# The convolution's result in two parts from where it is made to where it is used

## The chip, the cores and the metric

One core of one Trainium2 chip runs the whole program. The metric is the device time of one execution in microseconds (us); the smaller it is, the better. Matrix products run on TensorE (PE in the profile), elementwise work on VectorE (DVE) and ScalarE (ACT), and SyncE (SP) issues most transfers; ACT issues some too.

## The reference, cut to what matters

One encoder layer (model width 1024) is applied to two sequences of 1024 positions, the prompt and the sample, each with its own conditioning vector. A sequence is normed and projected to twelve operands; a gated short convolution gives `y_a`, a two-way gated linear attention with four heads gives `y_b`, and the two are merged under sigmoid gates:

```
proj = h @ w_in
(a_b, a_c, a_x, a_z, q, k, v, b_z, lr_f, lr_b, m_a, m_b) = split(proj)
u   = depthwise_conv(a_c * a_x, conv_w, conv_b)          # three taps
y_a = (a_b * u * silu(a_z)) @ w_a_out                    # <- the convolution's result is a_b * u * silu(a_z)
y_b = (attention(q, k, v, gates) * silu(b_z)) @ w_b_out
out = x + gate * ((sigmoid(m_a) * y_a + sigmoid(m_b) * y_b) @ w_out)
```

All of it is float32. The kernel does a product as three products of rounded parts: an operand is split in a high part, rounded to the format that TensorE multiplies (`F32R`), and the low part that is left, and hi*hi + hi*lo + lo*hi is summed.

## The kernel before

Work goes sequence by sequence: `projections(0)`, `mixers(0)`, a merge, then `projections(1)`, `mixers(1)` and the second merge. Everything is kept with features on the 128 partitions and the 1024 positions beside each other, in rows of 128x1024 (512 KB); a product is made in halves of 512 positions.

In `projections` the convolution's eight rows are made. Two rows at a time come out of four jobs (`conv_jobs`); the first row (`first_conv`, sequence 0 only) and the single ones (`last_conv_jobs`) are made apart. A job does a block of 256 features with seven block products instead of eight (`fast`), of 12 matmuls each, and in sequence 0 the weights' seven operands are made on the way: ACT casts the high part, DVE subtracts it for the low one, and one operand is a sum of two blocks (line 204 to 208: `s` by DVE, its high part by ACT, its low part by DVE). When a convolution row `u` is finished by its last multiplication (line 646, 669 or 746), ACT's queue stores it, unsplit, in the DRAM tensor `ta_d[s][ct]` (lines 647, 670, 747).

In `mixers` each of four heads goes through `attention`. Its first part is a chain over levels B = 1, 2, 4, ..., 64. At a level ACT copies the keys into `km` (line 931), PE makes 16 small products `pl<-Q,km` (line 903; the program has 8 instructions, the profile counts two for each), DVE copies those that a mask names into `AT` (line 936; ACT from B = 32 on, lines 940 and 941), and DVE multiplies `Q` (944), `K` (947) and `T` (949) by the level's decays. The next level's `km` needs the new `K`, its products also the new `Q`.

Between the steps of this chain a generator of dense products is advanced, `gates()` and then `first_out()`. The last group of `gates()` is two blocks of the merge gate, 96 matmuls in eight steps k. From k = 4 on, each step calls `reload`, which brings two rows of the convolution's result back: four loads of 256 KB (a half row each) into staging slots `raw` by the SP queue (line 117), and for each a cast `b<-raw` by ACT (line 122) and a subtraction `b<-raw,b` by DVE (line 123). A tile `b` holds the high and the low part of a row in one of 18 big slots (1 MB). `first_out()` is the product with `w_a_out`: 12 matmuls for each `b` in its first group (`ps<-b,w`, lines 141 to 143). The first group's four result banks are those of the gate's last group; ACT's sigmoids (line 764) free them.

The order on every engine is decided when the kernel is built by a scheduler with its own estimates; on the chip each engine works its list in order, and waits at an instruction whose operands are not there.

Of the kernel before, what the change touches and what calls it, by code (L numbers as in the profile page):

```python
# [11 lines left out]
F32 = mybir.dt.float32  # L12
F32R = mybir.dt.float32r
# [4 lines left out]
P = 128  # L18
D = 1024
KT = D // P  # L20
L = 1024
# [36 lines left out]
def encoder_kernel(ctx, tc, x_p, x_s, x_t, weights, w_lr, w_gate, w_out, vectors, b_gate, final_norm_g, masks, y_p, y_s):  # L58
    nc = tc.nc
# [9 lines left out]
    dram = ctx.enter_context(tc.tile_pool(name="dram", bufs=1, space=bass.MemoryType.DRAM))  # L69


    def big(name, dtype=F32, shape=(P, 2, L)):
        return sb.tile(list(shape), dtype, name=name, tag="big", bufs=NBIG)
# [29 lines left out]
    kept_d = dram.tile([36, 7, P, 2 * HALF], F32, name="kept_d")  # L103
    g_d = [dram.tile([2 * KT, P, L], F32, name=f"g_d{s}") for s in range(2)]
    m1_d = [dram.tile([KT, P, L], F32, name=f"m1_d{s}") for s in range(2)]
    ta_d = [dram.tile([KT, P, L], F32, name=f"ta_d{s}") for s in range(2)]
    ob_d = [dram.tile([KT, P, L], F32, name=f"ob_d{s}") for s in range(2)]
    mg_d = [dram.tile([P, KT, L], F32, name=f"mg_d{s}") for s in range(2)]
    r1_d = dram.tile([P, L], F32, name="r1_d")
# [7 lines left out]
        queue(nc.sync.dma_start(out=raw, in_=src))  # L117
        return raw

    def split(hi, lo, raw, engine):  # L120

        high = nc.scalar.copy(out=hi, in_=raw)  # L122
        engine.tensor_sub(out=lo, in0=raw, in1=hi.bitcast(F32))  # L123
        return high

    def load_w(i, w=None, **kw):
# [469 lines left out]
    def projections(s, mv, started):  # L596
        def tile_of(kind):

            made = {}

            def place(r, c):
                sl = slice(c * HALF, (c + 1) * HALF)
                if kind == "big":
                    if "t" not in made:
                        made["t"] = big("pair")
                    return made["t"][:, r, sl]
                if r not in made:
                    made[r] = small("single")
                return made[r][:, sl]

            return place

        whole = slice(0, L)

        def taps(ct, pr):

            w = [vecs[:, V_CW + 8 * i + ct:V_CW + 8 * i + ct + 1] for i in range(3)]
            u = small("u")
            nc.scalar.activation(out=u, in_=pr, func=AF.Identity, scale=w[1], bias=vecs[:, V_CB + ct:V_CB + ct + 1])
            for i, src, dst in ((0, slice(0, L - 1), slice(1, L)), (2, slice(1, L), slice(0, L - 1))):  # L620
                nc.vector.scalar_tensor_tensor(out=u[:, dst], in0=pr[:, src], scalar=w[i], in1=u[:, dst],
                                               op0=ALU.mult, op1=ALU.add)
            return u

        def row(place, r):
            a = place(r, 0)
            return bass.AP(a.tensor, a.offset, [list(a.ap[0]), [1, L]])

        def silu(z, sg):
            nc.scalar.activation(out=sg, in_=z, func=AF.Sigmoid)  # L630
            nc.vector.tensor_mul(out=z, in0=z, in1=sg)

        def conv_jobs(ct):
            pc, px, pz, pb = tile_of("big"), tile_of("big"), tile_of("small"), tile_of("small")
            us = {}

            def x_there(r):
                nc.vector.tensor_mul(out=row(pc, r), in0=row(pc, r), in1=row(px, r))
                us[r] = taps(ct + r, row(pc, r))

            def z_there(r):
                silu(row(pz, r), row(px, r))
                nc.vector.tensor_mul(out=us[r], in0=us[r], in1=row(pz, r))

            def b_there(r):
                nc.vector.tensor_mul(out=us[r], in0=us[r], in1=row(pb, r))
                nc.scalar.dma_start(out=ta_d[s][ct + r], in_=us[r])

            return [pair(w + ct, w + ct + 1, p, there) for w, p, there in (
                (W_AC, pc, lambda r: None), (W_AX, px, x_there), (W_AZ, pz, z_there), (W_AB, pb, b_there))]  # L650

        def last_conv_jobs(ct):

            p1, p2 = tile_of("big"), tile_of("big")
            u, done = [], []

            def cx_there(r):
                done.append(r)
                if len(done) == 2:
                    nc.vector.tensor_mul(out=row(p1, 0), in0=row(p1, 0), in1=row(p1, 1))  # L660
                    u.append(taps(ct, row(p1, 0)))

            def zb(r):
                done.append(r)
                if r == 0:
                    silu(row(p2, 0), row(p1, 1))
                    nc.vector.tensor_mul(out=u[0], in0=u[0], in1=row(p2, 0))
                if len(done) == 4:
                    nc.vector.tensor_mul(out=u[0], in0=u[0], in1=row(p2, 1))
                    nc.scalar.dma_start(out=ta_d[s][ct], in_=u[0])  # L670

            return [pair(W_AC + ct, W_AX + ct, p1, cx_there), pair(W_AZ + ct, W_AB + ct, p2, zb)]

        def out_job(i, dst, gate=None):

            p = tile_of("small")

            def there(r):
                if gate == "silu":
                    silu(row(p, r), small("sg"))  # L680
                elif gate:
                    nc.scalar.activation(out=row(p, r), in_=row(p, r), func=AF.Sigmoid)
                nc.scalar.dma_start(out=dst[r], in_=row(p, r))

            load, place, quarter = pair(i, i + 1, p, there)
            if W_V <= i < W_BZ:
                load.load = lambda n, kh: value_tile(i, n, kh)
            return load, place, quarter

        jobs = []  # L690
        if started:
            first_conv(s, mv, started, taps, silu)
        for ct in range(1, 7, 2):
            jobs += conv_jobs(ct)
        jobs += last_conv_jobs(KT - 1)
        n_conv = len(jobs)

        for w, d in ((W_Q, q_d), (W_K, k_d)):
            jobs.append(out_job(w, [d[s][r, :, 0, :] for r in range(2)]))
        for g in range(NH):  # L700
            jobs.append(out_job(W_V + 2 * g, [v_d[s][g, :, r, :] for r in range(2)]))
            jobs.append(out_job(W_BZ + 2 * g, [z_d[s][g, :, r, :] for r in range(2)], "silu"))
        for f in range(0, KT, 2):
            jobs.append(out_job(W_MA + f, [g_d[s][f + r] for r in range(2)], "sigmoid"))
        for n, (load, _, _) in enumerate(jobs):
            load.keep, load.ready, load.even = n, s == 1, n >= n_conv
        if not started:
            more = last_conv_jobs(0)
            jobs = more + jobs
            n_conv += len(more)  # L710
        steps = 7 * (len(jobs) - n_conv)
        side = chain(decays(s), gate_rows() if s else ())
        n_side = (1 + 9 * NH) + (KT + 1 + 2 if s else 0)
        owed = 0.0
        for n, _ in enumerate(fast(jobs, mv)):
            if s and n == 8:
                run(low_ranks(s, mv))
            if n + 1 >= 7 * n_conv:
                owed += 1.02 * n_side / steps
                while owed >= 1.0:  # L720
                    owed -= 1.0
                    next(side, None)
        run(side)

    def first_conv(s, mv, started, taps, silu):

        banks, sums_of = started
        pr, zs = small("pr"), [small("z") for _ in range(2)]
        z, sg = zs
        for ps, sl in banks[0]:  # L730
            nc.scalar.copy(out=pr[:, sl], in_=ps)
        for ps, sl in banks[1]:
            nc.vector.tensor_mul(out=pr[:, sl], in0=ps, in1=pr[:, sl])
        for ps, sl in banks[2]:
            nc.scalar.copy(out=z[:, sl], in_=ps)
        pb = small("pb")
        more = chain(halves(W_AB, lambda ps, sl: nc.scalar.copy(out=pb[:, sl], in_=ps), mv.act), low_ranks(s, mv))
        next(more)
        for k in range(4):
            sums_of(k)  # L740
            next(more, None)
        run(more)
        u = taps(0, pr)
        silu(z, sg)
        nc.vector.tensor_mul(out=u, in0=u, in1=z)
        nc.vector.tensor_mul(out=u, in0=u, in1=pb)
        nc.scalar.dma_start(out=ta_d[s][0], in_=u)
        mf = small("mf", shape=(P, len(MASKED), P))
        nc.sync.dma_start(out=mf, in_=masks)
        nc.vector.tensor_copy(out=mk, in_=mf)  # L750


    def mixers(s, mv):
        def gates():
# [18 lines left out]

            for k, _ in enumerate(group([(W_MA + i, gate(i)) for i in range(n, n + 2)], mv.act)):
                if k >= 4:
                    reload(ta_d[s], conv, (2 * k - 8, 2 * k - 7))
                yield

        conv = [None] * KT
# [360 lines left out]
    mv = Moving()  # L1140
    started = start(mv)
    projections(0, mv, started)
    mixers(0, mv)
    mv = Moving()
# [73 lines left out]
```

## Time and profile before

| | |
|---|---|
| median of 3 runs | 2373.42 us (2373.26 to 2377.82) |
| the profiled execution | 2377.87 us, span 2376.0 us |
| PE busy | 2301.9 us, 97% of the span |
| DVE busy | 1424.6 us, 60% |
| ACT busy | 1008.8 us, 42% |
| memory traffic | 294.90 MB read, 197.79 MB written, 207 GB/s over the span |

The span runs from the first to the last instruction; the time of the execution has 1.9 us more around it. A busy share close to one on PE means that time is lost or won almost only where PE stands, or where its clock is lower.

### The profile page before, as it was taken

How to read it: one execution, taken by the hardware profiler on the slowest of the kernel's cores; microseconds unless marked ns; L12 is line 12 of the kernel's file. 1: busy time of each engine (PE TensorE's matmuls, PEld its weight loads, DVE VectorE, ACT ScalarE, POOL GpSimd, SP SyncE). 2: the span in 40 equal slices, each digit the busy share in tenths (PEclk: the TensorE clock that was granted, in tenths of full speed). 3: DMA queues.
4: the chain of work that ended last, by engine and by line, in shares of the span. 5: the costliest groups of instructions: out<-in, count | busy, mean ns of one | idle time of the engine just before them, and what ended most of it. 6: DMA issues, size and time to landing. Idle time of an engine off the chain costs nothing.

```text
span 2376.0 us, 29248 instructions
## 1 busy us (share of the span) xinstructions
PE 2301.9 (97%) x10897; PEld 1883.3 (79%) x10897; DVE 1424.6 (60%) x2021; ACT 1008.8 (42%) x1655; POOL 34.3 (1%) x72
## 2 busy tenths in 40 slices
PE   7999999999999989999999999999999989999998
PEld 3688887887888868878788888888778878888887
DVE  4676676666576878868622332344476876965443
ACT  4443443666655546443421112555145544442221
POOL 0000000000000000000000000000000000000000
PEclk8999999999999999999999999999999999999999
DMA  6267767888863245557366667787853244478431
GB/s 234 71 245 282 268 252 279 314 298 302 308 235 110 99 146 201 211 184 245 113 202 212 212 201 230 256 277 269 306 187 113 101 150 169 160 246 300 154 124 62
DMA packets 189902, 494.63 MB, mean 208 GB/s; under 512 B 18912, under 2 KB 45632, under 8 KB 185664
## 3 DMA queue, kind: packets, MB, share of 16 engines
q1 hardware_dynamic: 166960, 405.98, 49.8%
q10 hardware_dynamic: 22800, 86.78, 9.4%
q8 instruction: 86, 1.41, 0.2%
q14 instruction: 56, 0.46, 0.1%
HBM read 294.90 MB, written 197.79 MB: 207 GB/s over the span
## 4 chain that ended last, share of the span: by engine, by line
PE 83%; DMA 7%; DVE 6%; ACT 2%; issue 1%; POOL 1%; SPq 0%; POOLq 0%; DVEq 0%; ACTq 0%
PE ps L141 9%; PE ps L143 9%; PE ps L142 9%; PE pl L277 8%; PE pl L278 8%; PE pl L279 8%; PE ps L278 6%; PE ps L279 6%; PE ps L277 6%; PE pl L903 3%; DMA raw<-in_weights_dram 2%; DMA qk<-q_d 2%; PE pm L141 1%; PE pm L142 1%; PE pm L143 1%
## 5 line engine op out<-in xcount | busy, mean ns | idle before, releaser
L123 DVE TENSOR_TENSOR w<-raw,w 128x512 fp32r<-128x512 f32 x298 | 202.2, 686 | 100.1 <-ACT w L122 99.1
L122 ACT CAST w<-raw 128x512 fp32r<-128x512 f32 x298 | 183.3, 621 | 161.7 <-PE ps L143 51.5
L277 PE MATMUL pl<-th,w 128*128 128x512 f32 x584 | 228.1, 391 | 1.1 <-ACT keep L282 1.1
L278 PE MATMUL pl<-tl,w 128*128 128x512 f32 x584 | 227.9, 390 | 0.0
L279 PE MATMUL pl<-th,w 128*128 128x512 f32 x584 | 227.6, 390 | 0.0
L141 PE MATMUL ps<-b,w 128*128 128x512 f32 x512 | 202.8, 396 | 0.4 <-ACT w L122 0.3
L142 PE MATMUL ps<-b,w 128*128 128x512 f32 x512 | 201.8, 394 | 0.2 <-DVE b L123 0.2
L143 PE MATMUL ps<-b,w 128*128 128x512 f32 x512 | 201.0, 393 | 0.0
L141 PE MATMUL ps<-hi,w 128*128 128x512 f32 x432 | 173.5, 402 | 1.7 <-ACT hi L390 1.7
L143 PE MATMUL ps<-hi,w 128*128 128x512 f32 x432 | 171.2, 397 | 1.5 <-DVE w L123 1.5
L142 PE MATMUL ps<-lo,w 128*128 128x512 f32 x432 | 170.7, 395 | 0.7 <-DVE lo L391 0.7
L282 ACT COPY keep<-pl 128x512 f32<-128x512 f32 x116 | 67.7, 584 | 242.2 <-PE pl L279 242.1
L278 PE MATMUL ps<-lo,w 128*128 128x512 f32 x352 | 138.2, 393 | 0.4 <-DVE lo L123 0.4
L279 PE MATMUL ps<-hi,w 128*128 128x512 f32 x352 | 137.8, 391 | 0.4 <-DVE w L123 0.4
L277 PE MATMUL ps<-hi,w 128*128 128x512 f32 x352 | 137.7, 391 | 0.3 <-ACT hi L122 0.3
L277 PEld LDWEIGHTS pl<-th,w 128*128 128x128 f32 x584 | 110.0, 188 | 24.9 <-ACT keep L282 1.7
L278 PEld LDWEIGHTS pl<-tl,w 128*128 128x128 f32 x584 | 109.9, 188 | 23.0
L279 PEld LDWEIGHTS pl<-th,w 128*128 128x128 f32 x584 | 109.8, 188 | 22.9
L903 PE MATMUL pl<-Q,km 128*128 128x128 f32 x768 | 101.8, 287 | 19.4 <-ACT km L931 14.5
L903 PEld LDWEIGHTS pl<-Q,km 128*128 128x128 f32 x768 | 95.3, 198 | 31.5 <-ACT km L931 20.1
L141 PEld LDWEIGHTS ps<-b,w 128*128 128x128 f32 x512 | 97.0, 189 | 19.3 <-ACT w L122 0.7
L142 PEld LDWEIGHTS ps<-b,w 128*128 128x128 f32 x512 | 96.9, 189 | 19.0 <-DVE b L123 1.0
(287 smaller groups left out, 5043.7 us busy)
## 6 DMA issues: line engine op xcount, KB each, us to landing
kept_d<-w SPq DMA_DIRECT2D x196, 512.0 KB, 4.1
raw<-in_weights_dram SPq DMA_DIRECT2D x256, 256.0 KB, 4.3
w<-kept_d SPq DMA_DIRECT2D x112, 512.0 KB, 3.4
wk<-kept_d SPq DMA_DIRECT2D x168, 256.0 KB, 3.1
g<-g_d SPq DMA_DIRECT2D x32, 512.0 KB, 4.6
araw<-in_weights_dram SPq DMA_DIRECT2D x16, 512.0 KB, 3.7
ta_d<-u ACTq DMA_DIRECT2D x16, 512.0 KB, 3.5
v_d<-single ACTq DMA_DIRECT2D x16, 512.0 KB, 5.2
```

What stands on the lines that cost most here:

```text
L122: high = nc.scalar.copy(out=hi, in_=raw)
L123: engine.tensor_sub(out=lo, in0=raw, in1=hi.bitcast(F32))
L141: nc.tensor.matmul(out, ahi, bhi, start=(first and i == 0), stop=False)
L142: nc.tensor.matmul(out, ahi, blo, start=False, stop=False)
L143: nc.tensor.matmul(out, alo, bhi, start=False, stop=(last and i == n - 1))
L277: nc.tensor.matmul(ps, whi[:, cs], mhi, start=(first and k == 0), stop=False, skip_group_check=True)
L278: nc.tensor.matmul(ps, whi[:, cs], mlo, start=False, stop=False, skip_group_check=True)
L279: nc.tensor.matmul(ps, wlo[:, cs], mhi, start=False, stop=(k == 3), skip_group_check=True)
L282: nc.scalar.copy(out=job[i, "keep"], in_=ps)
L903: nc.tensor.matmul(pl[:, j * P:(j + 1) * P], km[:, c * P:(c + 1) * P], qm(c), start=True, stop=True)
```

## The change

A row of the convolution's result is split at once where it is made: `keep_conv` lets ACT cast `u` into a spare row (one whose contents are used up: `z`'s row of the pair, or of the single row), lets DVE subtract the cast from `u` in place, and stores both, the high part and the low one, by two 512 KB transfers on ACT's queue. `ta_d` has two parts for each row. Where the row is wanted again, one 1 MB load on SP's queue brings both parts into a `b` tile; there is no staging slot, no cast and no subtraction.

```diff
-    ta_d = [dram.tile([KT, P, L], F32, name=f"ta_d{s}") for s in range(2)]
+    ta_d = [dram.tile([KT, 2, P, L], F32, name=f"ta_d{s}") for s in range(2)]
...
-    def split(hi, lo, raw, engine):
+    def split(hi, lo, raw, engine, hi32=None):
 
         high = nc.scalar.copy(out=hi, in_=raw)
-        engine.tensor_sub(out=lo, in0=raw, in1=hi.bitcast(F32))
+        engine.tensor_sub(out=lo, in0=raw, in1=hi.bitcast(F32) if hi32 is None else hi32)
         return high
...
+        def keep_conv(ct, u, spare):
+
+            split(spare.bitcast(F32R), u.bitcast(F32R), u, nc.vector, hi32=spare)
+            for i, t in enumerate((spare, u)):
+                nc.scalar.dma_start(out=ta_d[s][ct, i], in_=t)
...
             def b_there(r):
                 nc.vector.tensor_mul(out=us[r], in0=us[r], in1=row(pb, r))
-                nc.scalar.dma_start(out=ta_d[s][ct + r], in_=us[r])
+                keep_conv(ct + r, us[r], row(pz, r))
...
-                    nc.scalar.dma_start(out=ta_d[s][ct], in_=u[0])
+                    keep_conv(ct, u[0], row(p2, 0))
...
-        nc.scalar.dma_start(out=ta_d[s][0], in_=u)
+        keep_conv(0, u, z)
...
                 if k >= 4:
-                    reload(ta_d[s], conv, (2 * k - 8, 2 * k - 7))
+                    for f in (2 * k - 8, 2 * k - 7):
+                        conv[f] = big("b", F32R)
+                        nc.sync.dma_start(out=conv[f].bitcast(F32), in_=ta_d[s][f].rearrange("a p t -> p a t"))
                 yield
```

The scheduler places the rest anew. Lines below the diff's first insertion have other numbers in the changed kernel (903 becomes 911, 931 becomes 939, 764 becomes 770). PE's list at the third head's levels, where the convolution's rows come back, in the kernel before: behind the last products of the gate's group (`ps<-hi,w`, `ps<-lo,w`) stand the 24 of levels B = 4, 8 and 16 together, then the first ones with `b`.

```order
L141 MATMUL ps<-hi,w 128x512
L142 MATMUL ps<-lo,w 128x512
L143 MATMUL ps<-hi,w 128x512
L903 MATMUL pl<-Q,km 128x128 x24
L141 MATMUL ps<-b,w 128x512
L142 MATMUL ps<-b,w 128x512
```

The same place in the changed kernel, from the products of B = 4 on:

```order
L911 MATMUL pl<-Q,km 128x128 x8
L141 MATMUL ps<-hi,w 128x512
L142 MATMUL ps<-lo,w 128x512
L143 MATMUL ps<-hi,w 128x512
L141 MATMUL ps<-hi,w 128x512
L142 MATMUL ps<-lo,w 128x512
L143 MATMUL ps<-hi,w 128x512
L911 MATMUL pl<-Q,km 128x128 x8
L141 MATMUL ps<-b,w 128x512
L142 MATMUL ps<-b,w 128x512
L143 MATMUL ps<-b,w 128x512
```

Six matmuls of the gate's group now stand between B = 4 and B = 8; behind B = 8 come five with `b` (the last two, lines 141 and 142, are not shown), and then the eight of B = 16. It is the same in both sequences.

ACT's list at that place, before: `Xh` is the cast that opens the chain, `sg` are the gate's sigmoids that free PE's banks.

```order
L122 CAST Xh<-K 128x2048
L122 CAST b<-raw 128x512 x5
L913 COPY K<-qk 128x1024
L924 COPY AT<-pl 128x512 x2
L122 CAST b<-raw 128x512
L931 COPY km<-K 128x1024
L122 CAST b<-raw 128x512 x4
L931 COPY km<-K 128x1024
L122 CAST b<-raw 128x512 x4
L931 COPY km<-K 128x1024
L122 CAST b<-raw 128x512 x2
L931 COPY km<-K 128x1024
```

And now:

```order
L122 CAST w<-raw 128x512 x2
L122 CAST Xh<-K 128x2048
L921 COPY K<-qk 128x1024
L932 COPY AT<-pl 128x512 x2
L939 COPY km<-K 128x1024 x2
L122 CAST w<-raw 128x512 x2
L939 COPY km<-K 128x1024 x2
L770 ACTIVATE sg<-ps 128x512 x3
```

The 16 casts of `b` are gone, and four casts of the first weights of `w_a_out`, which stood behind the last `km` before, stand ahead. DVE's list loses its 16 subtractions for `b` there in the same way, and SP's list has eight loads `b<-ta_d` in place of sixteen `raw<-ta_d`, six of these slots' early turns being taken by weights.

DVE's list at the first convolution row of sequence 0, before, from the row's last multiplication on:

```order
L746 TENSOR_TENSOR u<-u,pb 128x1024
L123 TENSOR_TENSOR w<-raw,w 128x512
L204 TENSOR_TENSOR s_838<-raw 128x512
L289 TENSOR_TENSOR pair<-ps,keep 128x512
L206 TENSOR_TENSOR raw<-raw 128x512
L208 TENSOR_TENSOR w<-s_838,w 128x512
```

And now:

```order
L752 TENSOR_TENSOR u<-u,pb 128x1024
L123 TENSOR_TENSOR w<-raw,w 128x512
L204 TENSOR_TENSOR s_841<-raw 128x512
L123 TENSOR_TENSOR u<-u,z 128x1024
L206 TENSOR_TENSOR raw<-raw 128x512
L289 TENSOR_TENSOR pair<-ps,keep 128x512
L207 TENSOR_TENSOR raw<-s_841,raw 128x512
L292 TENSOR_TENSOR pair<-pl,pair 128x512
L208 TENSOR_TENSOR w<-s_841,w 128x512
```

The subtraction that makes the convolution row's low part, a full row, is in, and line 208, which makes the low part of a weights' operand, stands three instructions later.

## Rows read from the trace of the kernel before

**Rows 1.** PE's waits over the span: total us, times, longest.

```profile
PE pl L903 <- ACT km L931: 14.5, 6, 6.3
```

**Rows 2.** By tile, `b` and `ta_d`: ns min/median/max of both splits; who waited for loads.

```profile
L122 ACT CAST b<-raw x64: 610/618/661, 861.2 to 2124.1; 128x512 fp32r<-128x512 f32 x64
L123 DVE TENSOR_TENSOR b<-raw,b x64: 678/690/708, 863.5 to 2124.7; 128x512 fp32r<-128x512 f32 x64
...
  ACT b L122: 21.4, 14
```

**Rows 3.** PE's timeline, sequence 0, third head: start, duration, [idle before <-releaser].

```profile
873.64 0.39 PE L143 MATMUL ps<-hi,w 128*128 128x512 f32 x1
874.98 2.05 PE L903 MATMUL pl<-Q,km 128*128 128x128 f32 x16 [0.95 <-ACT km L931]
883.31 3.79 PE L903 MATMUL pl<-Q,km 128*128 128x128 f32 x16 [6.28 <-ACT km L931]
889.22 2.59 PE L903 MATMUL pl<-Q,km 128*128 128x128 f32 x16 [2.12 <-DVE Q L944]
891.46 0.77 PE L141 MATMUL ps<-b,w 128*128 128x512 f32 x1
...
893.74 0.47 PE L143 MATMUL ps<-b,w 128*128 128x512 f32 x1
```

**Rows 4.** ACT's timeline at the same place.

```profile
877.04 0.62 ACT L122 CAST b<-raw 128x512 fp32r<-128x512 f32 x1 [2.12 <-DMA raw<-ta_d]
...
882.22 1.04 ACT L931 COPY km<-K 128x1024 f32<-128x1024 f32 x1
...
889.25 1.56 ACT L764 ACTIVATE sg<-ps 128x512 f32<-128x512 f32 x3
```

**Rows 5.** DVE's timeline at the same place.

```profile
875.30 1.90 DVE L123 TENSOR_TENSOR b<-raw,b 128x512 fp32r<-128x512 f32 x3
877.11 1.34 DVE L936 COPY_PREDICATED AT<-mk,pl 128x512 f32<-128x512 uint8 x2
878.33 1.23 DVE L944 TENSOR_TENSOR Q<-Q,T 128x1024 f32<-128x1024 f32 x1
879.46 1.30 DVE L947 TENSOR_TENSOR K<-K,T 128x512 f32<-128x512 f32 x2
```

**Rows 6.** PE's timeline, sequence 1, third head, the same three levels.

```profile
1944.06 2.05 PE L903 MATMUL pl<-Q,km 128*128 128x128 f32 x16 [1.24 <-ACT km L931]
1951.10 3.78 PE L903 MATMUL pl<-Q,km 128*128 128x128 f32 x16 [4.99 <-ACT km L931]
1957.01 2.02 PE L903 MATMUL pl<-Q,km 128*128 128x128 f32 x16 [2.12 <-ACT w L122]
```

**Rows 7.** PE's timeline in sequence 0's projections, a wait and a matmul behind it.

```profile
414.67 0.70 PE L862 MATMUL pm<-lrs,wg 96*128 96x512 f32 x2 [2.23 <-DMA lrs<-lr_d]
...
416.18 0.63 PE L278 MATMUL ps<-lo,w 128*128 128x512 f32 x1
```

**Rows 8.** Windows: us, PE, PEld, DVE, ACT, POOL busy (count), PEclk, DMA share, GB/s.

```profile
200.00:300.00 100.00, 100.00 (x443) 82.83 (x442) 64.00 (x90) 37.34 (x62) 0.00 (x0) 1.00 0.75 275
...
884.25:886.50 2.25, 2.25 (x13) 2.25 (x12) 1.12 (x3) 0.97 (x2) 0.00 (x0) 0.50 0.97 258
...
1060.00:1080.00 20.00, 19.96 (x89) 16.17 (x88) 11.74 (x18) 5.05 (x9) 0.00 (x0) 1.00 0.93 327
```

**Rows 9.** First convolution row: DVE makes an operand's low part; PE's first use.

```profile
132.94 0.68 DVE L208 TENSOR_TENSOR w<-s,w 128x512 fp32r<-128x512 f32 x1
...
135.29 0.39 PE L279 MATMUL ps<-th,w 128*128 128x512 f32 x1
```

**Rows 10.** The same two instructions at a later pair of convolution rows.

```profile
205.99 0.68 DVE L208 TENSOR_TENSOR w<-s,w 128x512 fp32r<-128x512 f32 x1
...
211.45 0.39 PE L279 MATMUL ps<-th,w 128*128 128x512 f32 x1
```

**Rows 11.** PE's use of `vT`, third head of sequence 0: ns, first and last start.

```profile
L961 PE MATMUL pm<-ident,vT x16: 272/272/328, 907.7 to 911.7; 128*128 128x128 f32 x16
```

More of the change, by code (lines that the diff above doesn't have):

```diff
@@ L691, in projections @@
         if started:
-            first_conv(s, mv, started, taps, silu)
+            first_conv(s, mv, started, taps, silu, keep_conv)
         for ct in range(1, 7, 2):
@@ L723, in projections, with first_conv @@
         run(side)
-    def first_conv(s, mv, started, taps, silu):
+    def first_conv(s, mv, started, taps, silu, keep_conv):
         banks, sums_of = started
```

## The prediction

> **What bounds the kernel now.** The busy table comes first: PE is at work for 97% of the span, so other engines count only where PE stands. The list of PE's waits says where. Its largest entry is the products of the attention's levels waiting for ACT's copy `km`: 14.5 us in six waits [rows 1]. PE's timeline puts 13.5 of these 14.5 us at one place in each sequence, the first part of the third head, where the convolution's rows are loaded back. In sequence 0, PE waits 0.95, 6.28 and 2.12 us before levels B = 4, 8 and 16, which is 9.35 us [rows 3]; in sequence 1 it waits 1.24, 4.99 and 2.12, which is 8.35 us [rows 6].
>
> Next to read is what else PE loses there: its clock. Sixteen level products take 2.05 us at their best and 3.79 after the 6.28 us wait [rows 3], and the granted clock of that stretch is 0.50, the lower level, 1.2 GHz [rows 8]. Over sequence 0 that costs 3.79 - 2.05 = 1.7, then 2.59 - 2.05 = 0.5, then the first six matmuls with `b`: the last of them starts 2.28 us after the first [rows 3], against 5 x 0.226 = 1.13 at the usual spacing (100 us for 443 matmuls, [rows 8]), 1.1 more. Together 3.4 us. In sequence 1 it is 3.78 - 2.05 = 1.7 [rows 6].
>
> Last, the timelines of the two engines that the chain runs through. ACT's shows why `km` is late: casts `b<-raw` stand in front of it, and such a cast waits for its load [rows 4]; in all, ACT's casts for `b` wait 21.4 us, in 14 waits, for loads from `ta_d` [rows 2]. DVE is never idle long there, and subtractions for `b` stand between the level's own operations: three of them between 875.30 and 877.11, ahead of the copies into `AT` [rows 5]. So both engines of the chain are held up by the split on loading. The place costs 9.35 + 3.4 = 12.8 us in sequence 0 and 8.35 + 1.7 = 10.1 in sequence 1.
>
> **What is removed.** Per sequence, 16 casts of 0.62 us and 16 subtractions, which follow each other at (877.11 - 875.30) / 3 = 0.60 us [rows 5], 9.7 us of DVE time in a chain that is served by DVE and ACT in turn. The Trainium skill ("VectorE: DVE Perf Modes", the section on the TRN2 errata) says that an instruction pays a fixed time on top of its elements, which would make 512 elements 0.69 us. That is the duration in the row of the split, 0.69 [rows 2], but instructions queued behind each other start 0.60 us apart, so the spacing is what I count; by the page's figure the sum would free 11.1 us instead of 9.7 on DVE, and the chain below would be no shorter for it, as it counts only its own operations.
>
> **What the chain needs without them**, sequence 0, on the same clock times. PE's list now holds six of the gate's matmuls back until after B = 4, so PE comes to B = 4 at 873.64 + 0.23 - 6 x 0.226 = 872.5. Before, `km` for it was copied behind three waiting casts; with these and four subtractions (2.4 us) out of the way I count it as ready, no wait. The products take 2.05, to 874.6; the six matmuls cover PE to 875.9. In that time DVE has a half of the copies (0.61), `Q` (878.33 to 879.46, 1.13) and the second half of `K` (0.60) to do [rows 5], 2.34, to 876.9; then ACT's copy takes 1.04 [rows 4], and with two handovers of about 0.1 the products of B = 8 start at 878.1. **PE waits 2.2 us.** They end at 880.2. Next come five matmuls with `b`; their first bank is freed by the gate's first sigmoid, which ACT's list has behind the `km` of B = 16. That `km` waits for DVE: two weights' subtractions, `T` and two halves of `K` behind 876.9, 3.0 us, to 879.9; copy to 881.0; a third of 1.56 us for the first sigmoid [rows 4], 881.5. **PE waits 1.4 us.** The five take 1.1, to 882.7; B = 16 then finds its `Q` (879.9 + 1.22 + 1.13 = 882.3) and ends at 884.8. Before, PE was as far (B = 16 and five with `b` issued) at 893.74 [rows 3]. That is 8.9 us earlier.
>
> From this comes what the clock takes. A single wait of 2.23 us in the projections was followed by matmuls of 0.63 us instead of 0.39 [rows 7]; the 3.78 and 2.05 us of [rows 6] differ by 1.7 behind 4.99 us. I take 1.7 per sequence, with nothing and 3.4 as its ends. **Sequence 0 gains 8.9 - 1.7 = 7.2 us. Sequence 1** has the same order; it keeps 2.2 + 1.4 + 1.7 = 5.3 of its 10.1, **a gain of 4.8.**
>
> **The loads.** Eight of 1.05 MB instead of sixteen of 256 KB: 8.4 MB, twice the bytes. Their slots come free one after another; the latest is last read in the gate's step k = 5, and 24 matmuls follow that step, so it is free by 873.9 - 24 x 0.226 = 868.5 at the latest. At 327 GB/s, the rate of a stretch with the DMA engines busy 0.93 [rows 8], 8.4 MB take 25.7 us; even if nothing moved before 868.5 all is there by 894.2. PE wants the first `b` at 881.6 and each further one 12 x 0.226 = 2.7 us later, the eighth after 900. On the same bound the first lands at 871.7 (1.05 MB, 3.2 us). No wait, with 6 us in hand or more. At the 258 GB/s of the slow stretch [rows 8] the eight take 32.5 us, to 901: the eighth is then the first that could be late.
>
> **What is added in the projections.** For each of the 16 rows a cast of 1024 (ACT's copy of that size is 1.04, [rows 4]), a subtraction of 1024 (`Q` of that size 1.13 to 1.23, [rows 5]) and a second 512 KB store, with ACT's queue standing until the subtraction is done. PE has no idle there and DVE 36 us free of 100 [rows 8], so what matters is whether a weights' operand comes late. At the first row it does: the low part of the operand ends at 132.94 + 0.68 = 133.62 and is wanted at 135.29 [rows 9], 1.67 in hand; the full subtraction (1.13) and two 0.60 instructions now stand ahead of it, 2.33 us. **0.7 lost.** At the pairs there is 211.45 - 206.67 = 4.8 in hand [rows 10], against two subtractions, 2.3, and ACT held for about 1.9 (one of them and an instruction of 0.69 ahead of it): hidden, but with half a microsecond to spare if both add up. The extra 4.2 MB of stores in about 350 us are 12 GB/s on 275 [rows 8]. I put 1.0 for all of this, 0.7 and 3 as its ends.
>
> **Sum:** 7.2 + 4.8 - 1.0 = **11.0 us**. The profiled execution took 2377.87, at the upper end of the three runs, and would take 2366.9; from the median of 2373.42 it is **2362.4 us**. A measurement of this kernel can tell about 0.2%, 4.7 us, from no change.
>
> **Rivals.**
> - *All of the place is won* (12.8 + 10.1 - 1.0 = 21.9, 2351.5). It wants the DVE chain to keep ahead of PE at B = 8, which six matmuls (1.36 us) don't cover by the count above. 0.12.
> - *The wait stays in the chain.* Levels alternate PE, DVE, ACT, PE, and if the copies of B = 2 still come late, B = 4 waits 1.5 us more, B = 8 runs at the lower clock and with it `b`: 3.6 + 1.5 + 3.4 = 8.5 is left of each sequence, the gain 4.3 + 1.6 - 1.0 = 4.9, 2368.5; anything worse is within the bound. The 2.34 us of DVE operations per level, which the change doesn't touch, speak for it; the 21.4 us of waiting casts, which are gone, against. 0.16.
> - *SP's queue.* The loads of `g` (two of 512 KB) and `vT` (1 MB) now stand behind 8.4 MB. The Trainium skill ("DMA: Bandwidth & Descriptors", on queues, rings and completion order) has a DMA engine take a queue's work in the order of its ring; no row of before tests that. In rows: behind loads that end at 894.2 by the bound above, `vT` lands 2 x 3.2 later, at 900.6 at 327 GB/s; its first use, at 907.7 [rows 11], moves to 900.5 by the 7.2 us gained. The bound starts all eight loads at the last one's time; by the order six of the slots are free a step of 12 matmuls (2.7 us) sooner at least, which I take to leave it in time. At 258 GB/s from 2.7 us sooner it is 868.5 - 2.7 + 32.5 + 2 x 4.1 = 906.5, PE stands 6 us in sequence 0 and as long in sequence 1, and of the 11.0 gained nothing is left: 2374. 0.06.
> - *Slower: the projections' operands come late at the pairs.* With more than 4.8 us of added delay there PE waits, and what comes next is a clock drop. Were the six pair rows of sequence 0 late by 2.2 us each, as in [rows 7], with 1.6 of clock behind it (eight matmuls of twice the spacing), 6 x 3.8 = 23 us would be lost: 2362.4 + 23 = 2385. It becomes slower than before from 1.8 us a row on. For it speaks that ACT's list is in order and stands behind the second store; against it the 36% that DVE has free. 0.06.
>
> **The chances.** The forecast has 0.60, and its own range is 2357 to 2368: the ends of the clock (1.7 each way and sequence) and of the projections' 1.0. With the full gain on one side and the chain's wait on the other the range is **2351 to 2371**. Faster by over 0.2% (below 2368.7) are the forecast, the full gain and half of the third case: 0.80. Within 0.2%: the rest of it and the queue, 0.14. Slower by over 0.2%: 0.06.
>
> **What would show it.** In the changed kernel's trace PE should have no wait before B = 4, one of about 2 us before B = 8 put down to `km`, and one of 1 to 2 us before the first `b`, put down to a sigmoid; ACT's waits for `ta_d` should be gone, and PE should not wait for `b`'s loads. In the projections one new wait of about 0.7 us at an operand of line 208 near 135 us. I am wrong if PE waits over 3 us at B = 4 or B = 8, if it waits for loads of `b` or `vT`, or if more than a microsecond or two of new waits stand in the first 600 us.

## The result, and the profile after

The changed kernel takes 2356.57 us (median of 4, 2353.4 to 2362.86) against 2375.53 of the kernel before on the same chip: a ratio of 0.9922, 95% interval 0.9907 to 0.9937, 18.5 us faster. Two later comparisons of the same pair gave 0.9936 (0.9923 to 0.9949) and 0.9928 (0.9912 to 0.9945), 15 and 17 us. The profiled execution took 2362.86 us with a span of 2361.1, where the one of before had 2376.0: 14.9 us, and it is the slowest of the four. Two more executions of the changed kernel were profiled with the later comparisons, with spans of 2355.4 and 2357.2; of the kernel before there is the one.

PE's waits over the span: total us, times, longest.

```profile
PE pm L1054 <- DVE ot L1046: 11.6, 16, 2.5
PE pl L911 <- ACT km L939: 6.0, 4, 2.5
```

The 14.5 us of [rows 1] are 6.0 now. What was the second entry, the 16 waits for `ot` in the attention's last part, which the change doesn't touch, is the first. PE's timeline at the third head of sequence 0 shows levels B = 4 and 8, the first `b` and B = 16:

```profile
874.01 1.95 PE L911 MATMUL pl<-Q,km 128*128 128x128 f32 x16
879.82 3.61 PE L911 MATMUL pl<-Q,km 128*128 128x128 f32 x16 [2.48 <-ACT km L939]
883.26 0.50 PE L141 MATMUL ps<-b,w 128*128 128x512 f32 x1
...
885.46 2.02 PE L911 MATMUL pl<-Q,km 128*128 128x128 f32 x16 [0.79 <-DVE Q L952]
```

Against [rows 3], the waits are 0, 2.48 and 0.79 us instead of 0.95, 6.28 and 2.12. The sixteen products of B = 8 take 3.61 us, 1.6 over their 2.05. The same place in sequence 1, B = 8, the first `b` and B = 16 (B = 4 doesn't wait):

```profile
1939.52 2.05 PE L911 MATMUL pl<-Q,km 128*128 128x128 f32 x16 [2.48 <-ACT km L939]
1942.96 0.50 PE L141 MATMUL ps<-b,w 128*128 128x512 f32 x1 [1.38 <-ACT sg L770]
...
1944.22 1.95 PE L911 MATMUL pl<-Q,km 128*128 128x128 f32 x16
```

The same wait of 2.48 us before B = 8, but here its products run at full speed (2.05), and the wait for the sigmoid before the first `b` shows, 1.38. In sequence 0 the slow products hid it, and the later `Q` took its place. The third profiled execution bears this out: there the products of B = 8 take 2.05 us in sequence 0 too, and the wait for the sigmoid shows, 1.38. DVE's timeline there, sequence 0, behind the products of B = 4, answers to [rows 5]:

```profile
875.65 1.34 DVE L944 COPY_PREDICATED AT<-mk,pl 128x512 f32<-128x512 uint8 x2
876.88 1.21 DVE L952 TENSOR_TENSOR Q<-Q,T 128x1024 f32<-128x1024 f32 x1
878.01 0.68 DVE L955 TENSOR_TENSOR K<-K,T 128x512 f32<-128x512 f32 x1
```

and ACT's, for [rows 4]:

```profile
878.73 1.04 ACT L939 COPY km<-K 128x1024 f32<-128x1024 f32 x1 [0.73 <-DVE K L955]
```

Copies, `Q` and `K` follow each other on DVE with nothing between; `km` waits for `K` alone, and starts right behind it, at 878.73 where `K` ends at 878.69.

The waits don't tell all that the place gained. PE issues the same instructions there before and after, so the stretch from the first products of the third head's B = 2 to those of the fourth head's can be compared whole (us, then the busy time and the count of PE, PEld, DVE, ACT and POOL, granted clock, DMA share, GB/s). Before, sequence 0 and 1:

```profile
867.96:981.77 113.81, 99.89 (x534) 84.30 (x534) 93.74 (x146) 61.89 (x120) 2.40 (x4) 0.96 0.63 220
1936.87:2038.94 102.07, 92.07 (x505) 77.02 (x505) 80.95 (x125) 48.45 (x98) 2.40 (x4) 0.97 0.55 196
```

And after:

```profile
869.54:974.84 105.30, 97.94 (x534) 82.56 (x534) 84.09 (x130) 54.91 (x108) 2.40 (x4) 0.98 0.70 258
1929.26:2023.42 94.16, 89.27 (x505) 75.51 (x505) 71.22 (x109) 41.67 (x86) 2.40 (x4) 1.00 0.62 235
```

The two stretches fell from 215.9 us to 199.5, and to 198.6 and 198.4 in the two other profiled executions: 16.4 to 17.5 us are won there.

The loads in transfers: the window from 858 to 905 us in 40 slices of 1.2 us.

```profile
GB/s 244 0 0 12 225 356 415 408 429 415 429 404 418 404 404 418 404 418 394 401 425 401 401 363 373 436 429 418 418 411 451 364 282 94 0 0 14 37 197 174
```

They move at 363 to 451 GB/s in an unbroken stretch, 409 in the mean from 866 to 891 us, and PE waits for none. In sequence 0's projections PE has one new wait and a longer one (windows 60 to 200 us and 200 to 420):

```profile
PE ps L279 <- DVE w L208: 0.6, 1, 0.6
...
PE pm L870 <- DMA lrs<-lr_d: 3.1, 1, 3.1
```

The first is the operand at the first row. The second was 2.2 us before. All of PE's waits from 60 to 700 us are 10.0 us, and 9.4 and 9.8 in the other two profiled executions, where they were 8.0.

### The profile page after: what moved, and what is told of

Its sections match the earlier page's. It is cut to its first block, busy times and chain, and to the rows that moved or that the text cites. A ratio compares the mean times of both kernels' runs of the same rounds, so it can differ in the third digit from the quotient of the medians.

```text
span 2361.1 us, 29175 instructions
## 1 busy us (share of the span) xinstructions
PE 2296.8 (97%) x10897; PEld 1878.6 (80%) x10897; DVE 1423.5 (60%) x2005; ACT 1006.6 (43%) x1639; POOL 34.3 (1%) x72
## 4 chain that ended last, share of the span: by engine, by line
PE 82%; DMA 6%; DVE 5%; ACT 3%; issue 2%; SPq 1%; POOL 1%; POOLq 0%; DVEq 0%; ACTq 0%
PE ps L141 10%; PE ps L143 10%; PE ps L142 10%; PE pl L277 8%; PE pl L278 8%; PE pl L279 8%; PE ps L279 6%; PE ps L278 6%; PE ps L277 6%; PE pl L911 3%; DMA raw<-in_weights_dram 2%; PE pm L141 1%; DMA qk<-q_d 1%; PE pm L142 1%; PE pm L143 1%
## 5 line engine op out<-in xcount | busy, mean ns | idle before, releaser
L141 PEld LDWEIGHTS ps<-b,w 128*128 128x128 f32 x512 | 96.3, 188 | 21.0 <-ACT sg L770 1.6
L142 PEld LDWEIGHTS ps<-b,w 128*128 128x128 f32 x512 | 96.3, 188 | 18.6 <-DVE b L123 0.5
L143 PEld LDWEIGHTS ps<-b,w 128*128 128x128 f32 x512 | 96.3, 188 | 18.6
```

The source lines that it names most:

```text
L141: nc.tensor.matmul(out, ahi, bhi, start=(first and i == 0), stop=False)
L142: nc.tensor.matmul(out, ahi, blo, start=False, stop=False)
L143: nc.tensor.matmul(out, alo, bhi, start=False, stop=(last and i == n - 1))
```

## The experiments

The theory behind the prediction is that the split on loading held the level chain on both engines. The rivals: only ACT's casts with their waits for loads did; only DVE's time did; or PE's new list did, which the scheduler wrote anew when the split was gone.

**The changed kernel again**, two more times beside the others.

> The changed kernel once more, on the same chip as the three others, to size the differences: 15 us under the kernel before if the two profiled executions are right (span 2361.1 against 2376.0), 19 if the medians of four are.

> The changed kernel a third time, beside the two others: 0.992 to 0.995 of the kernel before.

Measured 0.9936 and 0.9928; the intervals are given above. The three comparisons agree within them; single executions differ by up to 12 us (2353.4 to 2365.7 over all of them), and so a difference of a few us between kernels is read from the trace rather than from one median: from waits, and from the two stretches of the third head where the work is the same.

**DVE's operations put back.**

```diff
                         nc.sync.dma_start(out=conv[f].bitcast(F32), in_=ta_d[s][f].rearrange("a p t -> p a t"))
+                        for t in range(2):
+                            lo = conv[f][:, 1, t * HALF:(t + 1) * HALF]
+                            nc.vector.tensor_tensor(out=lo, in0=lo.bitcast(F32), in1=lo.bitcast(F32), op=ALU.max)
```

> The changed kernel with DVE's time put back: each loaded b gets two DVE operations of 512 on its low part (a maximum of the part with itself, which changes nothing), 16 per sequence, in the places where the subtractions stood; ACT has no cast for b. PE's list is again that of the kernel before (17 matmuls of the gate's group, then the levels B = 4 and 8 together), as the scheduler reacts to DVE's load. Theory 1 (the level chain was held by both engines' work): DVE's 9.6 us per sequence in the chain make PE wait some 3 us at B = 4 and 5 at B = 8, most of the gain goes, 2364 to 2371. Theory 2 (only ACT's casts, which waited for loads in front of km, held the chain): DVE's operations fit in beside, PE's waits stay near those of the changed kernel, 2355 to 2360.

Measured: 2373.89 us, ratio to the kernel before 0.9985 (0.9974 to 0.9995). Of the gain 3.6 us (1.2 to 6.2) are left. PE's timeline, B = 4, B = 8 and the first `b` of sequence 0:

```profile
876.72 2.05 PE L914 MATMUL pl<-Q,km 128*128 128x128 f32 x16 [1.66 <-ACT km L942]
883.54 3.79 PE L914 MATMUL pl<-Q,km 128*128 128x128 f32 x16 [4.77 <-ACT km L942]
888.79 0.79 PE L141 MATMUL ps<-b,w 128*128 128x512 f32 x1 [1.46 <-ACT sg L770]
```

DVE and ACT of the same kernel in front of B = 8:

```profile
876.94 1.93 DVE L787 TENSOR_TENSOR b<-b 128x512 fp32r<-128x512 f32 x3
878.74 1.36 DVE L947 COPY_PREDICATED AT<-mk,pl 128x512 f32<-128x512 uint8 x2
881.09 1.32 DVE L958 TENSOR_TENSOR K<-K,T 128x512 f32<-128x512 f32 x2
...
882.44 1.04 ACT L942 COPY km<-K 128x1024 f32<-128x1024 f32 x1 [5.77 <-DVE K L958]
```

PE's waits are 1.66 + 4.77 + 1.46 = 7.9 us in sequence 0 (9.35 before), and the same in sequence 1. ACT has no casts for `b`, and stands idle 5.77 us for `K`. The two stretches of the third head, with as many PE instructions as above, take together:

```profile
sum 215.47, PE 193.91 PEld 163.30 DVE 173.56 ACT 96.58 POOL 4.79; mean PE 96.95 PEld 81.65 DVE 86.78 ACT 48.29 POOL 2.40
```

That is 215.5 us against 215.9 in the kernel before. DVE's operations alone bring the loss back. "Only ACT" falls.

**ACT's copies put back.**

```diff
                         nc.sync.dma_start(out=conv[f].bitcast(F32), in_=ta_d[s][f].rearrange("a p t -> p a t"))
+                        for t in range(2):
+                            hi = conv[f][:, 0, t * HALF:(t + 1) * HALF]
+                            nc.scalar.copy(out=hi, in_=hi.bitcast(F32))
```

> The changed kernel with ACT's work put back: each loaded b gets two ACT copies of 512 on its high part (already rounded, so they change nothing), 16 per sequence, which wait for the loads and stand partly in front of km as the casts did; DVE has no subtraction for b, and PE's list is nearly that of the changed kernel (six gate matmuls between B = 4 and 8, one with b between B = 8 and 16). Theory 1 (both engines held the chain): 16 x 0.52 = 8.3 us of ACT, of which some six copies (3 us) and their waits stand in front of the km of B = 4 and 8; 3 to 6 us per sequence lost, 2362 to 2368. Theory 2 (only ACT held it): all of the gain goes, 2370 to 2375. Theory 3 (DVE's time alone, and PE's list, made the gain): 2355 to 2359, as the changed kernel.

Measured: 0.9936 (0.9920 to 0.9953), the same as the changed kernel beside it, 0.9936. PE before B = 8 and B = 16, sequence 0, and ACT in front of the `km` of B = 8:

```profile
877.42 3.56 PE L914 MATMUL pl<-Q,km 128*128 128x128 f32 x16 [2.69 <-ACT km L942]
883.00 2.02 PE L914 MATMUL pl<-Q,km 128*128 128x128 f32 x16 [1.78 <-DVE Q L955]
...
875.29 1.13 ACT L787 CAST b<-b 128x512 fp32r<-128x512 f32 x2
876.33 1.04 ACT L942 COPY km<-K 128x1024 f32<-128x1024 f32 x1
```

The wait at B = 8 is 0.2 us longer than in the changed kernel, since two copies end just behind `K`; the waits of the place are 4.5 us in sequence 0 against 3.3. The two stretches take together:

```profile
sum 201.51, PE 187.79 PEld 159.28 DVE 155.48 ACT 111.69 POOL 4.81; mean PE 93.90 PEld 79.64 DVE 77.74 ACT 55.84 POOL 2.40
```

That is 2 to 3 us more than the changed kernel's 198.4 to 199.5, for 15 us more of ACT's work, and part of it is the clock, which was low behind B = 8 in both sequences; it doesn't show in the time of the execution. The theory that both engines' work held the chain asked 3 to 6 us per sequence, and falls at that price. One thing this run doesn't bring back is the casts' waiting: the whole rows had landed, and ACT waited 0.2 us for loads in all, against 21.4 in [rows 2]. What that waiting did can only be read from the kernel before. In sequence 0, DVE's `K` for B = 8 ends at 879.46 + 1.30 = 880.76 [rows 5], and `km` starts at 882.22 [rows 4], behind casts that had waited:

```profile
881.05 1.26 ACT L122 CAST b<-raw 128x512 fp32r<-128x512 f32 x2 [1.41 <-DMA raw<-ta_d]
```

So ACT's casts held `km` up by 1.5 us beyond `K` there, and by 0.4 us at the same level of sequence 1; at B = 4 it was 0.1 and 0.3. They ended about when DVE did, and might have held the chain nearly as long by themselves. No run has these waits without DVE's operations, and so this rival is left open.

**The list on PE without DVE's time.** DVE's operations and PE's old list came together, so the list was put back by itself, by priority for the last two steps of the gate's group:

```diff
+            def ahead(steps):
+                k = 0
+                while True:
+                    if k >= 6:
+                        with tc.high_priority(offset=100):
+                            go = next(steps, 1)
...
-            for k, _ in enumerate(group([(W_MA + i, gate(i)) for i in range(n, n + 2)], mv.act)):
+            for k, _ in enumerate(ahead(group([(W_MA + i, gate(i)) for i in range(n, n + 2)], mv.act))):
```

> The changed kernel with another list on PE and no added work: the last two steps of the gate's group are given priority, so that no gate matmul is left between B = 4 and B = 8 (18 stand ahead of B = 4, and its products and those of B = 8 follow each other, as in the kernel before). DVE has no operations for b. It tells DVE's time from PE's list, which came together in the run with DVE's operations put back. If DVE's time is the cause: the six matmuls no longer cover 1.4 us, the wait at B = 8 grows from 2.5 to about 4, 1.5 to 3 us per sequence with the clock, 3 to 6 us slower than the changed kernel. If the list is the cause: as with DVE's operations back, 10 us or more slower.

Measured: 0.9947 (0.9931 to 0.9963), some 2.6 us behind the changed kernel's 0.9936, within the intervals. PE's timeline, B = 8 and B = 32 of sequence 0:

```profile
877.51 3.43 PE L924 MATMUL pl<-Q,km 128*128 128x128 f32 x16 [3.88 <-ACT km L952]
...
889.57 2.05 PE L924 MATMUL pl<-Q,km 128*128 128x128 f32 x16 [0.92 <-ACT km L952]
```

The wait at B = 8 is 3.88 instead of 2.48, 1.40 more: the six matmuls' own 1.36 us, as expected. In all, the waits at the place are 9.1 us in the two sequences instead of 7.1. The list is worth some 2 us; it isn't what made the gain.

**Half of DVE's operations**, one for each `b` (the loop above over one half in place of two).

> The changed kernel with half of DVE's time put back, 8 operations of 512 on the low parts of b per sequence (4.8 us) instead of 16, one for each b, which change nothing. PE's list has again 17 gate matmuls ahead of B = 4 and none between B = 4 and 8. If DVE's time is the cause: between the list alone and all 16, about half of the 12 us that 16 operations took, 5 to 8 us slower than the changed kernel. If the list is the cause: as with all 16, 10 to 12 slower.

Measured: 0.9944 (0.9929 to 0.9959), 2 to 4 us behind the changed kernel and level with the list alone, where 5 to 8 us were expected. PE's timeline, B = 4, B = 8, the first `b` and B = 32 of sequence 0, one entry of PE's waits, and the two stretches together:

```profile
877.72 2.05 PE L914 MATMUL pl<-Q,km 128*128 128x128 f32 x16 [0.59 <-ACT km L942]
884.09 3.01 PE L914 MATMUL pl<-Q,km 128*128 128x128 f32 x16 [4.32 <-ACT km L942]
887.53 0.80 PE L141 MATMUL ps<-b,w 128*128 128x512 f32 x1 [0.43 <-ACT sg L770]
...
897.90 2.05 PE L914 MATMUL pl<-Q,km 128*128 128x128 f32 x16 [1.29 <-ACT km L942]
...
PE pm L1057 <- DVE ot L1049: 8.6, 16, 1.0
...
sum 204.48, PE 189.94 PEld 159.59 DVE 164.21 ACT 96.39 POOL 5.61; mean PE 94.97 PEld 79.80 DVE 82.11 ACT 48.20 POOL 2.81
```

At the place the waits are 6.6 us in sequence 0 and 4.9 in sequence 1, 11.5 together: between the list alone (9.1) and all 16 operations (15.8). The stretches, with one PE instruction fewer in the trace, take 204.5 us, 5 to 6 more than in the changed kernel, where all 16 operations took 16 to 17 more. So at the place it goes as expected. But the waits for `ot` fell from 11.6 to 8.6, since the scheduler's list moved there too, and that gives 3 us back. The sizes of DVE's two halves are therefore to be had from the stretches and not from the medians: the second half cost about twice the first.

**The projections' side**, from both ends. Without the split (the row is stored twice):

```diff
-            split(spare.bitcast(F32R), u.bitcast(F32R), u, nc.vector, hi32=spare)
-            for i, t in enumerate((spare, u)):
+            for i, t in enumerate((u, u)):
```

> The changed kernel without the cast and the subtraction where a convolution row is made: the row is stored twice, unsplit (what is left out is the split itself; the low part that is loaded later is the row again). All stores, loads and the order in the mixers stay. Theory 1 (the split is hidden there but for 0.6 us at the first row): 0.5 to 1.5 us faster than the changed kernel. Rival (casts and subtractions delay operands all along sequence 0's projections, in small pieces): 3 us or more faster.

and with it alone, by loading and splitting again as the kernel before does:

```diff
-                    for f in (2 * k - 8, 2 * k - 7):
-                        conv[f] = big("b", F32R)
-                        nc.sync.dma_start(out=conv[f].bitcast(F32), in_=ta_d[s][f].rearrange("a p t -> p a t"))
+                    reload(ta_d[s][:, 1], conv, (2 * k - 8, 2 * k - 7))
```

> The kernel before with the change's production side alone: the convolution row is cast and subtracted where it is made, and two 512 KB parts are stored, but what is loaded back later is still split there (the row itself is stored as one of the two parts, the low part goes to a spare row and to the other, and is not read). Theory 1: 0.5 to 1.5 us slower than the kernel before, from about 0.7 at the first row. Rival (stores and splits slow sequence 0's projections in many places): 3 us or more slower, with PE's waits in the first 600 us up by as much.

(As built, the subtraction is in place, as in the change, and what is loaded back and split again is the low part, not the row; the instructions are those that the text counts.) Measured: 0.9929 (0.9917 to 0.9941) without the split, 1.7 us ahead of the changed kernel beside it, and 1.0010 (0.9996 to 1.0023) with it alone, 2.4 us behind the kernel before; neither difference is clear of the noise. PE's waits for the operand of line 208, from 60 to 700 us, without the split and with it alone:

```profile
PE ps L279 <- DVE w L208: 0.8, 1, 0.8
```

```profile
PE ps L279 <- DVE w L208: 1.7, 2, 1.1
```

The second wait there, 0.6, is the one at the first row: it goes with the split and comes with it. The sum of PE's waits in that window is 8.0 and 8.5 us, against 8.0 in the kernel before. The rival of many late operands, 3 us or more, falls. The run with the split alone is also a second look at the loss: with the change's stores but the old loading, the two stretches of the third head take 216.5 us, as in the kernel before (215.9), and 199.7 without the split.

**Work moved to cover the rest.** The number of steps that the generator of dense products owes at the start sets how much of the gate's group is left at the third head:

```diff
-        owed = 2.0
+        owed = 0.0
```

> The changed kernel with the generator of dense products started two steps later in each sequence (the number of steps owed at the start is 0 instead of 2), so that at the third head 9 to 11 matmuls of the gate's group stand between one level's products and the next, from B = 4 to B = 16. Theory: what is left of the waits there (2.5 and 0.8 or 1.4 us in a sequence, and 1.6 of clock in sequence 0) goes: 4 to 7 us faster than the changed kernel. Rival: the two steps are missed at other levels or at a sequence's end, and nothing or less is won.

> The changed kernel with the generator of dense products started one step later (1 step owed at the start, where the changed kernel has 2 and the run before this one 0). At the third head 19, 9 and 3 gate matmuls and 5 with b stand between the levels. Theory: like 0 owed, between the changed kernel and that run or as fast, 2352 to 2360.

Measured: 0.9919 (0.9903 to 0.9935) for 0, 2354.98 us, the lowest median of all, 2 to 4 us ahead of the changed kernel's 0.9928 and 0.9936, within intervals that overlap; 0.9937 (0.9922 to 0.9952) for 1, nothing won. With 0, PE's timeline at B = 32 of sequence 0, and PE's waits for `ot`:

```profile
886.93 2.05 PE L911 MATMUL pl<-Q,km 128*128 128x128 f32 x16 [3.21 <-ACT km L939]
...
PE pm L1054 <- DVE ot L1046: 6.6, 12, 0.9
```

The waits at B = 4, 8 and 16 are gone, but one of 3.21 stands at B = 32, in both sequences: 6.4 us against 7.1. What is won in waits at the place is 0.7 us, and the 1.6 of clock in sequence 0; the waits for `ot` fell by 5.0 us. If the time moved at all, it was mostly for another reason than the one stated.

The same with the kernel before:

> The kernel before, with its casts and subtractions on loading, and the generator started two steps later (0 owed instead of 2), so that 12 and 8 gate matmuls stand between the levels B = 2, 4 and 8. If the change's gain is DVE's time in a chain with too little beside it on PE, other work beside it wins part of that without the change: the chain of the kernel before takes 8.3 and 5.9 us for two levels there and 8 to 12 matmuls cover 1.8 to 2.7 each; 3 to 8 us faster than the kernel before, and the change would be worth some 10 to 15 us on top. If ACT's waits for its loads make the gain, it stays within 2 us of the kernel before.

Measured: 0.9975 (0.9962 to 0.9989), 6 us faster. That is within what was expected, and again not where: `ot` gives 4.6 us (6.9 against 11.5). PE's timeline at the place, B = 16, B = 32 and a `b`, in sequence 0, and the same `b` in sequence 1:

```profile
878.95 2.70 PE L903 MATMUL pl<-Q,km 128*128 128x128 f32 x16 [2.99 <-ACT km L931]
883.67 3.61 PE L903 MATMUL pl<-Q,km 128*128 128x128 f32 x16 [2.01 <-ACT sg L764]
890.57 0.79 PE L141 MATMUL ps<-b,w 128*128 128x512 f32 x1 [3.29 <-ACT w L122]
...
1950.36 0.79 PE L141 MATMUL ps<-b,w 128*128 128x512 f32 x1 [5.43 <-ACT w L122]
```

With more beside them the levels B = 4 and 8 don't wait at all, where B = 8 alone waited 6.28; B = 16 and 32 wait 2.99 and 2.01, and matmuls with `b` wait 3.29 and 5.43 us for casts of weights by ACT. In front of the 3.29 us' cast stands one cast of `b`, which doesn't wait for its load. In front of the cast that ends the 5.43 us, ACT itself waits for a load of weights:

```profile
1949.69 0.62 ACT L122 CAST w<-raw 128x512 fp32r<-128x512 f32 x1 [1.12 <-DMA raw<-in_weights_dram]
```

Why these weights come late was not tested. With the change in, the run with 0 owed has no such wait. Since the place itself didn't gain (its waits are 21.6 us in the two sequences, where they were 17.7), this run does not tell DVE's time from ACT's waits.

## Why the prediction was right

Direction and range held: 2356.57 lies in 2351 to 2371, and the gain, forecast as 11.0 us, is 15 to 18.5. Step by step:

- *Where the loss was.* Right. The two places gave 16.4 to 17.5 us, and no entry among PE's waits at other places moved by over 2 us.
- *"So both engines of the chain are held up."* Shown for DVE, whose operations alone brought back all but 3.6 us (1.2 to 6.2) of the gain, and all of it at the place. Wrong for ACT's work, whose copies alone cost 2 to 3 us at the place and nothing in the time. Not tested for the 21.4 us of casts that wait for loads: while DVE was as slow, they added 1.5 us to the wait for `km` at B = 8 of sequence 0 and 0.4 in sequence 1. The sum was made from DVE's chain, and so this hardly reached the number.
- *The chain without the split.* Waits of 0, 2.2 and 1.4 us were forecast; 0, 2.48 and 0.79 came in sequence 0 and 0, 2.48 and 1.38 in sequence 1. The releasers were `km` before B = 8 and, in sequence 1, the sigmoid before the first `b`, as said. The two handovers, put at 0.1 us each without a row for them, took 0.04 and 0.05.
- *The clock*, 1.7 us left per sequence. Sequence 0 kept 1.6 in two of the three profiled executions and none in the third; sequence 1 kept none in any: behind the same wait of 2.5 us its products took 2.05. This is one term that was mis-sized. By waits and clock, 9.35 + 3.4 - 3.27 - 1.6 = 7.9 us in sequence 0 (7.2 forecast) and 10.1 - 3.86 = 6.2 in sequence 1 (4.8), 14.1 instead of 12.0.
- *The size of the place.* Mis-sized too. Start to start the stretches gave 8.5 and 7.9 us, 16.4. The 2.3 beyond the 14.1 are smaller waits that the sum left out, 1.2 in all (0.74 us for `Vl`, a low part that DVE makes, in sequence 0, 0.28 for weights and 0.20 in sequence 1), and about 1 us of PE's busy time in sequence 1 that was not followed further.
- *The projections*, 1.0: 0.6 at the first row, where 0.7 was forecast, and 1.4 to 2.0 in all of PE's waits from 60 to 700 us in the three profiled executions. That is the edge of what the prediction itself named as a sign of being wrong. Half of it is a wait for `lrs`, 3.1 us instead of 2.2, and 3.0 and 3.2 in the other two. The run without the split has 2.5, the one on the kernel before with the split 2.2, so what the wait hangs on is open.
- *The loads.* No wait, as said, and with more in hand: 409 GB/s instead of the 327 counted. `vT` wasn't waited for; the rival of the queue did not come.
- *What is left.* The place less the projections is 14.4 to 15.9 us in the three profiled executions; their spans are 14.9, 20.6 and 18.8 below the one of before. Some of the rest lies ahead of anything that the change touches: the last product of line 454 starts at 91.43 us before and at 87.38, 89.85 and 88.34 after, while it does so at 88.76 in the kernel before with 0 owed. So single executions differ by some us there, and the 15 to 18.5 us of the medians need no further cause, though with one profiled execution of before that is not shown.

The number was nearer than its terms: the place was put some 5 us too low and the projections 0.4 to 1.0 too low, and the two partly cancel.

The rival "all of the place is won" (a gain of 21.9) was nearer in time than the forecast in two of the three comparisons, but not in kind: 7.1 us of waits are still there.

## What to carry to other kernels

Where a chain passes between engines, count for each the time of what isn't the chain's own: an engine without gaps, here DVE, holds it, while one that waits a great deal in it, here ACT, may only be waiting beside it. Put each engine's time back by itself before calling it the cause, and see whether its waits come back too. Work that can be done once where there is slack (a split where a value is made) should not stand in a chain, even if it doubles the bytes, as long as the transfers have room. Where two kernels issue the same instructions between two points, the time from start to start sizes a change better than a list of waits. And a scheduler's list changes elsewhere too: before an experiment's time is read as its edit's, look for waits that moved at places that the edit doesn't touch, as those for `ot` did here.

## What the runs showed of the hardware

- The clock after a wait. The same wait of 2.48 us at the same place of the program left the clock low in sequence 0 and high in sequence 1. The changed kernel's windows, during the products of B = 8 in both sequences, and the 5.7 us ahead of them (us, PE, PEld, DVE, ACT, POOL busy, granted clock, DMA share, GB/s):

```profile
880.00:883.00 3.00, 3.00 (x15) 3.00 (x16) 2.36 (x4) 1.34 (x2) 0.00 (x0) 0.50 1.02 408
1939.60:1941.60 2.00, 1.97 (x16) 1.78 (x16) 2.00 (x4) 0.24 (x1) 0.00 (x0) 1.00 1.02 406
...
874.10:879.80 5.70, 3.24 (x23) 2.64 (x21) 5.60 (x9) 2.28 (x3) 0.00 (x0) 0.99 1.02 407
1933.80:1939.50 5.70, 3.24 (x23) 2.63 (x21) 5.60 (x9) 2.28 (x3) 0.00 (x0) 1.00 1.02 405
```

  The granted clock is 0.50, 1.2 GHz, in one and 1.00, 2.4 GHz, in the other, and PE had been busy for the same 3.24 us of the 5.7 ahead of both. The second profiled execution shows the same pair (3.58 and 2.05 us for the products), but in the third the clock stays high in sequence 0 as well, behind 2.51 us:

```profile
877.42 2.05 PE L911 MATMUL pl<-Q,km 128*128 128x128 f32 x16 [2.51 <-ACT km L939]
```

  So it doesn't hang on the sequence, and a wait of this size has no fixed price: in the six cases it cost 1.6 us or so twice and nothing four times. What decides was not found.
- One core loaded 8.4 MB, and the transfers behind them, at 409 GB/s in the mean over 25 us, with a DMA share of 1.02, while PE and DVE worked; the stretch in [rows 8] had 327 at a share of 0.93.

```profile
866.00:891.00 25.00, 21.73 (x119) 18.39 (x118) 23.24 (x34) 10.17 (x14) 0.00 (x0) 0.93 1.02 409
```
